# A 512-byte store ahead of the first large store on the ScalarE queue

## The chip, the core and the metric

The kernel runs on one core of one Trainium2 chip. Its time is the device time of one execution, in microseconds (us); the median of three runs is given. A profile of one execution says what each engine and each DMA queue did. The engines that matter here are ScalarE (ACT, squares and roots), VectorE (DVE, sums) and SyncE (SP, which issues most DMA transfers); the transfers themselves run on 16 DMA engines.

## The reference

The kernel is an Lp pooling with p = 2 and windows of 4: of each four neighbours along the last axis it gives the root of the mean square. The input is 32 x 256 x 4096 in float32 (134.22 MB), the output a quarter of it (33.55 MB).

```python
for i in range(out_length):
    window = np.abs(x[:, :, 4 * i:4 * i + 4]) ** p
    result[:, :, i] = np.mean(window, axis=-1) ** (1.0 / p)
```

## The kernel before

Input and output are taken as flat arrays, cut into blocks, each laid out as 128 partition rows. A load brings a tile of 128 rows by W = 13184 columns into one of three input tiles (`x_tiles`, 6592 KB a load); 20 loads cover the input, load 3 being 32 columns narrower and load 19 shorter. Six blocks of loads, `[0..3]`, `[4..7]`, `[8..11]`, `[12..15]`, `[18, 16, 17]` and `[19]`, each end in one store: store 0 holds the results of loads 0 to 3, and so on.

For each load i the work is: ScalarE squares the tile in place (`square`, L89); VectorE adds pairs (`pairs`, L95) and then pairs of these (`fours`, L99) into the output tile `ot`, or, for loads 4, 8, 12 and 16, into a PSUM tile `st`; ScalarE takes the root of a quarter of the sums (`root`, L102). The output tile has four places, one for each load of a block, and is used again by each of the first four blocks.

The order of instructions on each engine is written out by hand: there is a manual schedule, and each engine runs its own list in order. The loop at L130 gives, for each load, any roots that are due ahead of its square (`ahead`), the square, any roots due behind it (`behind`), the two sums, and then the issue of load i + 3, which goes into the input tile that has just become free. For i = 3 the roots behind the square are those of loads 0 to 2, in one instruction over 9,888 columns. For i = 4 the root of load 3 goes ahead of the square, and `roots` (L106 to L116) then calls `store(0, nc.scalar)`.

Loads are issued from SyncE's queue (L83), which the profile calls q1. Stores 0, 1 and 2 are issued from ScalarE's queue (L86), which the profile calls q10; a store stands in ScalarE's list, so squares behind it in the list are issued after it. Stores 3, 4 and 5 are issued from SyncE. Semaphores make an instruction wait for the data it needs: a load for the sums that read its tile last, a sum into `ot` for the store that reads the old results, and a DMA for an earlier DMA that writes the same bytes. DMA transfers count on eight semaphores that are handed out in turn (lanes).

Near the end some of the squares of loads 18 and 19 are done by VectorE (L155), and the last three stores follow their roots.

## Time and profile before

| what | value |
| --- | --- |
| median of 3 runs (lowest, highest) | 394.09 us (393.97, 394.21) |
| profiled execution | span 392.3 us (392.26), from first to last instruction; the page gives no other time for it |
| read from HBM, written | 134.22 MB, 33.55 MB; 428 GB/s over the span |
| ScalarE busy | 274.4 us (70%) |
| VectorE busy | 218.2 us (56%) |
| chain that ended last, shares | DMA 43%, ScalarE 30%, VectorE 23% |
| a square of a full tile, its pairs, its fours | 11.19, 7.03, 3.59 us |
| a load, one after the other (squares 1, 2 and 3 start at 34.35, 49.94 and 65.47 us) | 15.5 to 15.6 us |
| stores 0, 1, 2 from issue to landing | 36.3, 35.2 and 35.0 us, shared with loads |

The profile divides the span into 40 slices of 9.8 us; digits are tenths of busy time, and the rate row is in GB/s. In the timeline, a row gives start, length, engine, line, operation, written and read tile, and in brackets how long the engine had been idle and what ended that. In the chain of work that ended last, each row is the start and length of a piece and what it was; a piece of DMA runs from the issue of a transfer to its landing, queueing included. "issue" is time in which the engine waited for nothing that the profile shows. The letter q behind an engine's name marks its DMA queue.

### The profile page before, as it was taken

The page shows a single profiled execution, that of the slowest core. Times are in us where ns is not written, and L with a number is a line of the kernel's source. Part 1 is how long each engine was busy: PE and PEld are TensorE (multiplying, and loading weights), DVE is VectorE, ACT ScalarE, POOL GpSimd, SP SyncE. Part 2 cuts the span into 40 slices and gives each one's busy share as a digit, 9 for nine tenths or more (in the row PEclk, how much of TensorE's full clock was granted, in tenths as well). Part 3 has the DMA queues.
Part 4 walks back from the last instruction along what each step waited for, and adds up shares of the span by engine and source line. Part 5 has one row for each costly group of instructions (what it writes and reads, how often), then busy time and mean ns, then how long its engine had stood idle before and what let it go on. Part 6 is the DMA issues. An engine that isn't in the chain of part 4 may idle for free.

```text
span 392.3 us, 176 instructions
## 1 busy us (share of the span) xinstructions
DVE 218.2 (56%) x42; ACT 274.4 (70%) x37; POOL 0.2 (0%) x4
## 2 busy tenths in 40 slices
DVE  0009477580693274905942748069418485699970
ACT  1095695979950859799509597995098999969910
POOL 0000000000000000000000000000000000000000
DMA  8999999999999999999999999999999999999997
GB/s 344 430 430 430 430 440 435 452 457 366 430 430 430 430 430 430 430 441 446 452 446 441 436 430 436 430 430 430 430 430 430 430 430 430 430 453 415 430 413 342
DMA packets 3744, 167.77 MB, mean 428 GB/s; under 512 B 416, under 2 KB 416, under 8 KB 416
## 3 DMA queue, kind: packets, MB, share of 16 engines
q1 hardware_dynamic: 3312, 147.53, 87.4%
q10 hardware_dynamic: 432, 20.25, 11.9%
HBM read 134.22 MB, written 33.55 MB: 428 GB/s over the span
## 4 chain that ended last, share of the span: by engine, by line
DMA 43%; ACT 30%; DVE 23%; issue 0%; ACTq 0%; SPq 0%; DVEq 0%
DMA xt<-in_x_dram 43%; ACT xt L89 28%; DVE xt L95 14%; DVE ot L99 5%; DVE xt L99 3%; DVE xt L155 2%; ACT ot L102 2%; ACT xt L102 1%; ACTq L86 0%; SPq L83 0%; DVEq L95 0%
## 5 line engine op out<-in xcount | busy, mean ns | idle before, releaser
L89 ACT ACTIVATE xt<-xt 128x13184 f32<-128x13184 f32 (+3 forms) x20 | 216.7, 10847 | 92.3 <-DMA xt<-in_x_dram 91.0
L95 DVE TENSOR_TENSOR xt<-xt 128x6592 f32<-128x6592 f32 (+2 forms) x20 | 139.7, 6985 | 144.1 <-ACT xt L89 143.9
L99 DVE TENSOR_TENSOR ot<-xt 128x3296 f32<-128x3296 f32 (+1 forms) x13 | 46.7, 3592 | 17.9 <-DMA out_dram<-ot 17.6
L102 ACT ACTIVATE ot<-ot 128x6592 f32<-128x6592 f32 (+3 forms) x8 | 37.2, 4655 | 7.0 <-DVE ot L99 7.0
L102 ACT ACTIVATE xt<-xt 128x3296 f32<-128x3296 f32 (+1 forms) x3 | 8.5, 2836 | 8.8 <-DVE xt L99 8.8
L99 DVE TENSOR_TENSOR st<-xt 128x3296 f32<-128x3296 f32 x4 | 14.4, 3600 | 0.1
L99 DVE TENSOR_TENSOR xt<-xt 128x3296 f32<-128x3296 f32 (+1 forms) x3 | 10.4, 3461 | 0.1
L102 ACT ACTIVATE ot<-st 128x3296 f32<-128x3296 f32 x3 | 8.7, 2898 | 0.0
L155 DVE TENSOR_TENSOR xt<-xt 128x4608 f32<-128x4608 f32 (+1 forms) x2 | 7.2, 3593 | 0.0
L102 ACT ACTIVATE xt<-st 128x3296 f32<-128x3296 f32 x1 | 2.9, 2898 | 0.0
L102 ACT ACT_TABLE_LOAD x1 | 1.3, 1283 | 0.7 <-PEq L189 0.7
L102 ACT ACTIVATE first<-const-float32-1.0 128x1 f32<-128x1 f32 x1 | 0.2, 202 | 0.0
L189 POOL MEMSET const-bfloat16-1.0<- 128x1 bf16 x1 | 0.1, 101 | 0.0
L189 POOL MEMSET const-uint8-127<- 128x1 uint8 x1 | 0.1, 101 | 0.0
L189 POOL MEMSET const-float32-0.0<- 128x1 f32 x1 | 0.1, 98 | 0.2 <-issue 0.2
L189 POOL MEMSET const-float32-1.0<- 128x1 f32 x1 | 0.1, 98 | 0.0
## 6 DMA issues: line engine op xcount, KB each, us to landing
xt<-in_x_dram SPq DMA_DIRECT2D x18, 6592.0 KB, 29.8
out_dram<-ot ACTq DMA_DIRECT2D x2, 6592.0 KB, 35.1
out_dram<-ot SPq DMA_DIRECT2D x1, 6592.0 KB, 37.1
out_dram<-ot ACTq DMA_DIRECT2D x1, 6588.0 KB, 36.3
xt<-in_x_dram SPq DMA_DIRECT2D x1, 6576.0 KB, 24.7
xt<-in_x_dram SPq DMA_DIRECT2D x1, 5840.0 KB, 21.9
out_dram<-xt SPq DMA_DIRECT2D x1, 4944.0 KB, 16.1
out_dram<-xt SPq DMA_DIRECT2D x1, 1460.0 KB, 8.2
```

The costliest lines, as they stand in the source:

```text
L89: return nc.scalar.activation(out=v, in_=v, func=Act.Square)
L95: return nc.vector.tensor_tensor(out=h, in0=q[:, :, 0:2], in1=q[:, :, 2:4], op=add)
L99: return nc.vector.tensor_tensor(out=o, in0=h[:, :, 0], in1=h[:, :, 1], op=add)
L102: return nc.scalar.activation(out=o, in_=s, func=Act.Sqrt, scale=1.0 / k)
L155: nc.vector.tensor_tensor(out=v, in0=v, in1=v, op=mybir.AluOpType.mult)
L189: nc = _bacc.Bacc("TRN2", target_bir_lowering=False, num_devices=1)
```

## The change

In the turn of the loop for load 3, behind the root of loads 0 to 2 and ahead of the root of load 3, ScalarE issues one more DMA: 128 floats (512 bytes) of partition row 0 of the output tile go to the first 128 floats of the output. These are results of load 0, so the values are the right ones; store 0 writes the same bytes again with the rest of its block. ScalarE's list has one instruction more. Store 0 gets one wait more, for the small store's completion, since both write the same bytes. The lanes of all later transfers move on by one. Nothing changes in the lists of the other engines.

```diff
         for group in behind.get(i, []):
             roots(*group)
+        if i == 3:
+            nc.scalar.dma_start(out=rows(of, 0, k)[0:1, 0:128], in_=o_tile[0:1, 0:128])
         sums[i] = pairs(xs[i]), fours(summed[i], xs[i])
         if i + X_SLOTS < n:
             load(i + X_SLOTS)
```

## The prediction

> **What bounds the kernel now.** I read the page first, then the table of busy time and DMA rate by stretch, then the timeline around the edit, then the chain that ended last.

> ```profile
> span 392.3 us, 176 instructions
> ...
> DMA  8999999999999999999999999999999999999997
> GB/s 344 430 430 430 430 440 435 452 457 366 430 430 430 430 430 430 430 441 446 452 446 441 436 430 436 430 430 430 430 430 430 430 430 430 430 453 415 430 413 342
> DMA packets 3744, 167.77 MB, mean 428 GB/s; under 512 B 416, under 2 KB 416, under 8 KB 416
> ...
> q1 hardware_dynamic: 3312, 147.53, 87.4%
> q10 hardware_dynamic: 432, 20.25, 11.9%
> ```

> The DMA engines are busy in every slice while ScalarE and VectorE have gaps, so up to the last landings the transfers set the time. The packet line gives the anatomy. There are 26 transfers; 416 small packets are 16 for each, and the other 3,328 are 128 for each: one packet for each partition row, eight on each of the 16 engines, and one small completion packet an engine. q1 carries SyncE's transfers, q10 ScalarE's three stores. One figure in the rate row stands out: 366 in the tenth slice (88 to 98 us), where q10 is used for the first time.

> ```profile
> 65.47:90.30 24.83, 16.91 (x4) 22.44 (x3) 0.00 (x0) 1.00 1.01 435
> 90.30:95.30 5.00, 0.00 (x0) 4.57 (x1) 0.00 (x0) 1.00 1.02 359
> 95.30:128.86 33.56, 19.80 (x4) 17.70 (x3) 0.00 (x0) 1.00 0.99 429
> 128.86:144.41 15.55, 5.77 (x2) 11.19 (x2) 0.00 (x0) 1.00 1.00 434
> 144.41:222.22 77.81, 42.50 (x9) 55.98 (x7) 0.00 (x0) 1.00 1.00 434
> ```

> The columns are the stretch, its length, busy time of VectorE, ScalarE and GpSimd, the clock, DMA share and rate. In the 5 us behind the first store's issue the engines call themselves full yet move 359 instead of 434 GB/s. The stretch from 65.47 to 144.41 (first four rows, 78.94 us) and that from 144.41 to 222.22 (77.81 us) each hold four loads and one store. So the first use of q10 costs **1.13 us of transfer time**. The packet records agree: a row takes 1.947 us, but around 92 us each of the 16 engines has one q1 row of 2.61 to 3.11 us just ahead of its first q10 row, 0.66 to 1.16 us too much, different for each. The second and third stores show no such row.

> ```profile
> 76.54 8.43 ACT L102 ACTIVATE ot<-ot 128x9888 f32<-128x9888 f32 x1
> ...
> 83.71 3.59 DVE L99 TENSOR_TENSOR ot<-xt 128x3288 f32<-128x3288 f32 x1
> 87.33 2.94 ACT L102 ACTIVATE ot<-ot 128x3288 f32<-128x3288 f32 x1 [2.36 <-DVE ot L99]
> 90.31 0.38 ACTq L86 DMA_DIRECT2D out_dram<-ot  x1
> 90.73 22.27 ACT L89 ACTIVATE xt<-xt 128x13184 f32<-128x13184 f32 x2 [0.46 <-ACT ot L102]
> ...
> 126.71 3.59 DVE L99 TENSOR_TENSOR ot<-xt 128x3296 f32<-128x3296 f32 x1 [6.65 <-DMA out_dram<-ot]
> 128.86 11.19 ACT L89 ACTIVATE xt<-xt 128x13184 f32<-128x13184 f32 x1 [15.86 <-DMA xt<-in_x_dram]
> ```

> These are the place of the edit and what is behind it. The root of loads 0 to 2 ends at 84.97; ScalarE then idles 2.36 us until load 3's sum. Store 0 is issued at 90.31.

> ```profile
> 90.73 21.94 ACT xt L89 x2
> 112.67 31.71 DMA xt<-in_x_dram
> 144.38 0.02 issue
> ```

> The chain runs from squares 4 and 5 to load 7's issue at 112.67, but most of the 31.71 us behind it is queueing: load 7 stands behind load 6 (landed by 128.86), then takes 15.55 us of its own.

> **The change, part by part.**

> *Issue.* One more DMA instruction on ScalarE, at about 85.0. Issues there take 0.34 to 0.38 us and end inside the 2.36 us gap, so root 3 still starts at 87.33: nothing. Without the gap it would cost that 0.38 us.

> *Data.* One row of 512 bytes is, by the one-packet-a-row count, one packet on one engine, against 128 packets on 16. At a row's rate (52,736 bytes in 1.947 us) 512 bytes are 0.02 us, and a 4-byte packet takes 0.01 us. The far bound is a whole row's place, 1.95 us on that engine. I take 0.03 us, by the small packets, the nearer row.

> *The first-use stall.* No row shows a one-row store. Below, the 1.13 us vanish (-1.13); above, the small store stalls its engine and store 0 stalls all again (+1.16). I take 0. The stall sits on each engine separately and with its own length, right ahead of that engine's first q10 row, which reads as a price for each engine and queue. The small store then pays on its one engine at about 87 to 89 us, the other fifteen pay at store 0, and each pays once. An early payment is no cheaper, since the engines are full from 65.47 on, and every load needs all sixteen. Even if the other fifteen were spared, loads would wait for the one that paid. That would gain at most the spread between engines, 0.6 us at the last load, since that one may have been ahead.

> *The added wait.* Store 0 now waits for the small store's landing. The second and third stores needed 3.4 us from issue to their first row, the first 4.5. The rows of two queues alternate on an engine (3.4 plus 16 x 1.947 gives 34.6, and 35.0 to 35.2 is measured), so the completion packet comes one q1 row later. The small store lands 3.4 + 1.95 = 5.3 to 4.5 + 1.95 = 6.4 us after 85.0, at 90.3 to 91.4, and ScalarE waits 0 to 1.1 us beyond 90.31. Bounds: none at all, or 2.9 us by the shortest store on the page (1,460 KB, 8.2 us, landing at 93.2). I take 1.1. The second semaphore adds a wait instruction, 0.02 us in SyncE's rows.

> Queued behind it on ScalarE are store 0 and squares 4 and 5; behind these are the sums of loads 4 and 5, the issues of loads 7 and 8 on SyncE, and VectorE's sum at 126.71, which waits for store 0. What hides it: load 7 is issued at 112.67 and load 6 occupies q1 until 128.86; load 8 is issued at 126.71 + 3.59 = 130.30 and load 7 occupies q1 until 144.41. Take off 3.4 us of start-up, and the shorter cover is 144.41 - 130.30 - 3.4 = **10.7 us**. Store 0 starting later only lets loads 5 and 6 run faster meanwhile. So 1.1 us of wait costs nothing on the path; beyond 10.7 us every further microsecond would count. The loads' lane waits that shift by one semaphore fall on transfers that landed long before, and SyncE and GpSimd issue nothing new.

> *Sum.* 392.26 + 0.03 + 0 + 0 = 392.3 us of span. The page gives no time for the profiled execution beyond its span; the median 394.09 lies 1.8 us above it, so I forecast **394.1 us**.

> **The rivals.**

> *The stall is gone (faster).* If the first use is paid once for the whole ScalarE queue, and 512 bytes are too few to hold up the loads behind them, store 0 starts as smoothly as the second store. That gives 394.09 - 1.13 + 0.03 = 393.0 us. For it: all 16 stalls fall within 4 us, and the first store's issue is also the longest of the three (0.38 against 0.34). Against it: lengths differ by engine, and a stall of the small store on a full engine is on the path too. Chance 0.23.

> [...]

> *The stall is paid twice (slower).* [...] Chance 0.20.

> *The wait becomes the bound (slower).* If the small store took as long as store 0 did (36.3 us), it would land at 121.3, hold ScalarE 31 us, and 31 - 10.7 = 20 us would show: 414 us. Against it: those 36 us are sixteen alternating rows, and it has one. Chance 0.03.

> *It warms nothing.* All sixteen engines stall at store 0 as before: 394.1, part of the forecast.

> **How the numbers follow.** Forecast 0.54, with its own range of 393.7 to 394.5 (spread gained, or the wait's remainder). A measurement of this kernel can tell about 0.2% (0.8 us) from no change, and the forecast lies inside that; the stall gone is faster (0.23), the other two slower (0.20 + 0.03). The range takes in 393.0 and 395.0 with 0.1 to 0.2 us at each side: 392.9 to 395.2; it leaves out the long wait and the outer parts of the stall lengths.

> **What would show it.** Right: one 512-byte packet on q10 ahead of store 0; store 0 issued near 91.4; in its first 5 us still a rate near 360 GB/s; squares 7 and 11 near 144.4 and 222.2. The stall gone: about 430 GB/s there and square 7 near 143.3. [...] The wait as bound: a ScalarE wait of over 10 us at store 0. What would make it wrong: a first-use price that does not belong to each engine alone.

## The result, and the profile after

The changed kernel takes 403.88 us (402.67 to 404.28, four runs), against 394.06 us before: a ratio of 1.0245, 95% interval 1.0233 to 1.0257. The forecast was no change. The profiled execution took 404.28 us with a span of 402.5 us, 1.8 us around it as before.

The same lines of the page of the changed kernel:

```profile
span 402.5 us, 178 instructions
...
DMA  8999999999999999999999999999999999999996
...
DMA packets 3746, 167.77 MB, mean 417 GB/s; under 512 B 417, under 2 KB 418, under 8 KB 418
...
q10 hardware_dynamic: 434, 20.25, 12.4%
```

Two packets more on q10, one of data (512 bytes, 0.027 us) and one of completion (4 bytes, 0.009 us): the small store is a single row on a single engine, as forecast. The engines are still busy in every slice. They move as many bytes (167.77 MB), but at 417 instead of 428 GB/s, and the 10.2 us more of span are that.

Where the rate is lost is read from stretches between the starts of squares 3, 7, 11, 14 and 17, which wait for their loads. First the changed kernel (columns as in the prediction), then the kernel before:

```profile
65.50:150.01 84.51, 42.51 (x9) 55.90 (x6) 0.00 (x0) 1.00 1.00 406
150.01:230.65 80.64, 42.42 (x9) 55.99 (x7) 0.00 (x0) 1.00 1.00 422
230.65:294.45 63.80, 34.57 (x7) 44.80 (x6) 0.00 (x0) 1.00 1.00 423
294.45:341.19 46.74, 28.12 (x6) 44.69 (x6) 0.00 (x0) 1.00 1.00 433
```

```profile
65.47:144.41 78.94, 42.48 (x9) 55.90 (x7) 0.00 (x0) 1.00 1.00 428
144.41:222.22 77.81, 42.50 (x9) 55.98 (x7) 0.00 (x0) 1.00 1.00 434
222.22:284.49 62.27, 36.81 (x8) 44.80 (x6) 0.00 (x0) 1.00 1.00 434
284.49:331.25 46.76, 25.85 (x6) 44.70 (x7) 0.00 (x0) 1.00 1.00 433
```

The three stretches with a store on ScalarE's queue are longer by 5.57, 2.83 and 1.53 us, 9.9 of the 10.2 us; the fourth, without one, is not longer. The change touches store 0 alone, yet stores 1 and 2 are slower too. The timeline around the edit:

```profile
85.03 0.51 ACTq L144 DMA_DIRECT2D out_dram<-ot  x1
87.35 2.94 ACT L102 ACTIVATE ot<-ot 128x3288 f32<-128x3288 f32 x1 [2.36 <-DVE ot L99]
92.59 0.37 ACTq L86 DMA_DIRECT2D out_dram<-ot  x1
93.00 22.27 ACT L89 ACTIVATE xt<-xt 128x13184 f32<-128x13184 f32 x2 [2.70 <-DMA out_dram<-ot]
...
134.41 11.19 ACT L89 ACTIVATE xt<-xt 128x13184 f32<-128x13184 f32 x1 [19.14 <-DMA xt<-in_x_dram]
```

The issue at 85.03 is hidden, and root 3 starts as before. The small store lands at 92.50, so store 0 is issued at 92.59, **2.28 us** later than the 90.31 of before. Load 6 is issued by SyncE, as before, and yet lands 5.5 us later (square 6 at 134.41 instead of 128.86). The chain names the small store but not the loss:

```profile
85.03 7.48 DMA out_dram<-ot
...
93.00 21.95 ACT xt L89 x2
114.94 35.04 DMA xt<-in_x_dram
```

ScalarE's 2.3 us are passed on to load 7's issue (114.94 instead of 112.67); the rest is inside the last piece, 35.04 us instead of 31.71, although load 7 had 2.3 us less to queue.

The packet records show where the time goes. Each packet is put behind the one that ended where it starts, which gives 16 sequences, one for each engine; the records do not number the engines, and a few sequences can't be followed to their end. L is a row of a load, S of a store, c the completion packet of a load (4 bytes, 0.009 us), with start times in us and, in brackets, lengths over 2.1 us; most of the other rows take 1.947 us. Two engines before, then two after:

```
L91.9(3.1) L95.0 S96.9 c98.8 S98.9 L100.8 S102.7 L104.7 S106.6
L92.1(2.9) S95.0 L96.9 S98.9 c100.8 S100.8 L102.8 S104.7 L106.7

L91.9 L93.9(2.1) c96.0 L96.0(2.8) S98.8 L100.8 S102.7(2.1) L104.9 S106.8(2.4)
L92.2 L94.2(2.4) S96.6 c98.5 S98.5 L100.5 S102.4 L104.4 S106.3
```

Before, store 0's first row goes ahead of load 5's completion on all 16 engines. After, it still does so on one engine, and on two it comes right behind the completion; on the other 13, load 5 has ended and exactly one row of load 6 has gone ahead. Below, a store is called n rows behind on an engine when n rows of the new load stand between the old load's completion and the store's first row. The 13 engines that are one row behind are the slow ones: from the store's first row to its last, load rows between included, they take 2.2 to 2.3 us a row.

### The profile page after: what moved, and what is told of

Read it like the earlier page. It is cut to its first block, busy times and chain, and to the rows that moved or that the text cites. A ratio compares the mean times of both kernels' runs of the same rounds, so it can differ in the third digit from the quotient of the medians.

```text
span 402.5 us, 178 instructions
## 1 busy us (share of the span) xinstructions
DVE 218.2 (54%) x42; ACT 274.4 (68%) x37; POOL 0.2 (0%) x4
## 2 busy tenths in 40 slices
DMA packets 3746, 167.77 MB, mean 417 GB/s; under 512 B 417, under 2 KB 418, under 8 KB 418
## 3 DMA queue, kind: packets, MB, share of 16 engines
q1 hardware_dynamic: 3312, 147.53, 86.3%
q10 hardware_dynamic: 434, 20.25, 12.4%
## 4 chain that ended last, share of the span: by engine, by line
DMA 46%; ACT 31%; DVE 20%; issue 0%; ACTq 0%; SPq 0%; DVEq 0%
DMA xt<-in_x_dram 44%; ACT xt L89 28%; DVE xt L95 12%; DVE ot L99 4%; ACT ot L102 3%; DVE xt L99 3%; DMA out_dram<-ot 2%; DVE xt L157 2%; ACT xt L102 1%; ACTq L86 0%; SPq L83 0%; DVEq L95 0%
## 5 line engine op out<-in xcount | busy, mean ns | idle before, releaser
L89 ACT ACTIVATE xt<-xt 128x13184 f32<-128x13184 f32 (+3 forms) x20 | 216.7, 10848 | 102.4 <-DMA xt<-in_x_dram 98.9
L99 DVE TENSOR_TENSOR ot<-xt 128x3296 f32<-128x3296 f32 (+1 forms) x13 | 46.7, 3591 | 32.9 <-DMA out_dram<-ot 32.5
L102 ACT ACTIVATE ot<-ot 128x6592 f32<-128x6592 f32 (+3 forms) x8 | 37.2, 4656 | 7.0 <-DVE ot L99 7.0
L99 DVE TENSOR_TENSOR st<-xt 128x3296 f32<-128x3296 f32 x4 | 14.4, 3600 | 0.1
L102 ACT ACTIVATE xt<-xt 128x3296 f32<-128x3296 f32 (+1 forms) x3 | 8.5, 2837 | 8.6 <-DVE xt L99 8.6
L99 DVE TENSOR_TENSOR xt<-xt 128x3296 f32<-128x3296 f32 (+1 forms) x3 | 10.4, 3462 | 0.1
L102 ACT ACTIVATE ot<-st 128x3296 f32<-128x3296 f32 x3 | 8.7, 2897 | 0.0
L102 ACT ACTIVATE xt<-st 128x3296 f32<-128x3296 f32 x1 | 2.9, 2898 | 0.0
L102 ACT ACTIVATE first<-const-float32-1.0 128x1 f32<-128x1 f32 x1 | 0.2, 203 | 0.0
```

Source lines behind the costliest of these rows:

```text
L89: return nc.scalar.activation(out=v, in_=v, func=Act.Square)
L99: return nc.vector.tensor_tensor(out=o, in0=h[:, :, 0], in1=h[:, :, 1], op=add)
L102: return nc.scalar.activation(out=o, in_=s, func=Act.Sqrt, scale=1.0 / k)
```

## The experiments

They stand in the order of the questions. The kernels that only delay a store do so by short activations into unused columns of the PSUM tile, ahead of the root that the store waits for. The second diff shows the first of these kernels; the others differ in the number of activations and their columns.

**Is it the small store, or the wait for it?**

The small store goes to store 5's block, so that store 5 takes the wait over:

```diff
+        if i == 3:
+            nc.scalar.dma_start(out=rows(of, 5, k)[0:1, 0:128], in_=o_tile[0:1, 0:128])
```

> The same small store, but to the first bytes of store 5's block, so that store 5, late, has the wait and store 0 has none; everything else as in the changed kernel. Theory 'late store' (the 2.28 us by which store 0 starts later set how the 16 engines fall between load rows and store rows, and that slows all three stores): store 0 is issued near 90.3 again and the time is near before, 394 to 396 us. Rival 'one engine' (a packet on one engine puts its queue out of step with the other fifteen): 402 to 405 us, as with the change.

Measured: 394.07 us, ratio 1.0001 (0.9990 to 1.0012); store 0 was issued at 90.54. The transfer itself, 0.027 us in the changed kernel, costs nothing that shows. In the next kernel there is no small store, only the delay:

```diff
+        if i == 3:
+            for _ in range(7):
+                nc.scalar.activation(out=s_tile[:, R:R + 508], in_=o_tile[:, 0:508], func=Act.Sqrt)
```

> No small store; seven short activations ahead of the root of load 3 (into unused columns of the PSUM tile) hold ScalarE so that store 0 and square 4 come some 2.3 us later. Theory 'late store': 402 to 405 us, with rows of 2.1 us and more during all three stores on ScalarE's queue. Rival 'one engine': 394 to 395 us, since the wait has 10 us of cover.

Measured: 400.75 (profiled) and 403.82 us, ratio 1.0208 (1.0115 to 1.0300).

```profile
92.35 0.38 ACTq L86 DMA_DIRECT2D out_dram<-ot  x1
```

Store 0 is 2.0 us late, there is no small store, and most or all of the loss is there: the late store 0 is enough, and the theory of one engine falls.

**What about a late store 0 is slow?**

> As the run with 2.3 us, but store 0 only some 0.3 us later. The rows of an engine take 1.947 us, and 2.28 is one such row and 0.33 us. If the theory 'late store' goes by the place within a row, this run is slow too, 400 us or more; if it goes by the distance to the end of load 5 or by the length of the wait, 394 to 395 us. Rival 'one engine': 394 us.

Four activations of 519 columns. Measured: 394.09 us, ratio 1.0003 (0.9991 to 1.0014); store 0 at 90.48, only 0.17 us late, so this tells little.

> As the run with 2.3 us, but store 0 some 1.95 us later, one whole row. If the theory 'late store' goes by the place within a row, this run is as before, 394 us; if it goes by the end of load 5 or the length of the wait, 400 us or more. Rival 'one engine': 394 us.

Six of 574. Measured: 394.19 us in the profiled execution and 403.43 in the other, of which no trace is kept, so this decides nothing by its time. In the profile store 0 was issued at 92.17, and all 16 engines put the first store row ahead of load 5's end. At 92.35 (the kernel with seven activations) three of 16 missed it and had a row of load 6 first, and these three took 2.2 us a row, the other 13 engines 1.95. That suggested the next theory, that engines on both sides of load 5's end disturb each other.

> No small store; store 0 some 1.0 us later than before (near 91.3), between the run that was fast at 0.1 us and the ones that were slow, or now slow and now fast, at 1.7 and 2.0 us. Theory 'straddle' (slow when some engines take their first store row ahead of load 5's last completion and some behind it, fast when all sixteen are on one side): all sixteen still ahead, 394 us. Rival 'longer wait': the time grows with the lateness, so 396 to 400 us.

Five of 579. Measured: 394.21 us, ratio 1.0001 (0.9989 to 1.0014), store 0 at 91.56; all 16 ahead, as both sides of the theory "straddle" wanted.

> No small store; store 0 some 3.1 us later than before (near 93.4), later than with the change. Theory 'straddle': by now all sixteen engines finish load 5 first and begin the store behind it, so it is fast again, 394 to 395 us, though it waits longer. Rival 'longer wait': 404 us or more.

Eight of 591. Measured: 404.78 us, ratio 1.0273 (1.0243 to 1.0303), store 0 at 93.83.

```profile
95.30:125.00 29.70, 17.65 (x3) 21.22 (x2) 0.00 (x0) 1.00 1.03 391
```

The rate in this stretch is 428 GB/s in the kernel before and 383 in the changed one. Nine engines had one row of load 6 first, seven had two. "Straddle" falls: none is ahead of load 5's end, and it is slow. On the nine, a store row takes 2.28 us; on the seven, 1.95 us.

> The changed kernel, with its small store and store 0's wait for it, and besides short activations ahead of the root of load 3, so that store 0 comes some 3.1 us later than before instead of 2.3. Theory 'straddle': as the run without the small store at the same place, 394 to 395 us, 9 us faster than the changed kernel for doing more work. Rival 'longer wait': 404 us or more. If this is slow and the run without the small store fast, the small store itself has a part.

The changed kernel and seven of 623. Measured: 405.48 us in both runs, ratio 1.0291 (1.0261 to 1.0321), store 0 at 93.53. With the small store or without, about the same; here all 16 engines are one row behind load 6.

**Is it the order of load 6 and store 0?**

The changed kernel, its wait kept, with load 6 issued behind store 0:

```diff
             roots(*ahead[i])
+        if i == 4:
+            nc.scalar.activation(out=s_tile[:, R:R + 16], in_=x_tiles[0][:, 0:16], func=Act.Sqrt)
+            load(6)
...
-        if i + X_SLOTS < n:
+        if i + X_SLOTS < n and i != 3:
```

> The changed kernel with its small store and its wait, but load 6 is issued behind store 0 (a 16-column activation behind store 0's issue reads load 6's tile, and load 6 waits for it), so that store 0's first rows come ahead of load 6's though store 0 is as late as with the change. Theory 'order' (slow when load 6's rows have begun before store 0's): 394 to 396 us. Rival 'late start' (the time of the start alone, against the rest of the kernel, counts): 402 us or more.

Measured: 394.09 us in the middle of eight runs (393.80 to 394.35, and one of 399.13), ratio 1.0021 (0.9983 to 1.0058). Timeline and rate of the profiled run:

```profile
92.46 0.37 ACTq L86 DMA_DIRECT2D out_dram<-ot  x1
...
93.09 39.76 SPq L83 DMA_DIRECT2D xt<-in_x_dram  x3
```

```profile
95.30:125.00 29.70, 17.65 (x3) 19.95 (x2) 0.00 (x0) 1.00 0.98 426
```

Store 0 is as late as with the change (92.46), load 6 is issued later too, and all of the loss is gone (the execution of 399.13 us has no trace). On nine engines store 0's first row now stands ahead of load 5's completion, on seven right behind it, and its rows take 1.95 us. So it is the order of rows, not the lateness.

> No small store; store 0 some 5 us later than before, so that load 6 is two or three rows ahead of it on each engine (one or two in the slow run at 3.1 us). Theory 'order': slow, 400 to 406 us. If it is fast, it is not the order alone but how many rows load 6 is ahead.

Ten of 656, store 0 at 95.50. Measured: 394.21 us median, but from 393.76 to 403.76 over nine runs. In the profiled run (397.79 us) all 16 engines had two rows of load 6 first, and store 0's rows took 1.95 us: so "one ahead is slow" did not hold for two. Its loss came later, at store 2, which gives the clearest view of all. There one engine had one row of the new load first; on the other 15 the store began ahead of the completion. The one, and one of the 15:

```
L249.8 c251.8 L251.8 S253.9 L255.9 S257.8(2.7) L260.5 S262.4(2.7) L265.1 S267.1(2.7)
L248.1 L250.1 S252.0 c254.0 S254.0 L255.9 S257.9 L259.8 S261.8 L263.7 S265.7 L267.6
```

The one engine writes most of its rows in 2.7 us (2.54 on the mean), beside 15 that need 1.95. So the store rows go by each engine's own sequence. Where many engines are slow, though, load rows of the others grow as well: in the run with store 0 at 93.83, the seven engines that are two rows behind take 1.95 us for a store row but 2.3 us for a load row between.

> No small store; store 0 some 8 us later than before, load 6 four rows ahead of it; still inside the cover of 10.7 us. Theory 'order': slow, 400 to 406 us. The run with 128 small rows ahead of store 0 (load 6 five or six rows ahead, 394.5 us) speaks for a return to 394 to 395 us at some number of rows; this run and the one at 5 us tell where.

Fourteen of 661, store 0 at 98.55, 8.2 us late. Measured: 394.24 us, ratio 1.0010 (0.9999 to 1.0022), four rows of load 6 first on 15 engines. Waiting 8 us costs nothing; waiting 2.3 to 3.5 us costs about 10.

> The changed kernel with its small store and its wait, and activations that hold store 0 until some 8 us later than before, 6 us later than with the change. Theory 'one row behind': four rows of load 6 are ahead, so rows take 1.95 us and the time is 394 to 395 us, some 9 us faster than the changed kernel for waiting longer. Rival 'late start': 404 us or more.

The changed kernel and fourteen of 618. Measured: 394.39 us, ratio 1.0007 (0.9996 to 1.0019).

```profile
98.64 0.37 ACTq L86 DMA_DIRECT2D out_dram<-ot  x1
```

```profile
95.30:125.00 29.70, 14.26 (x3) 27.31 (x5) 0.00 (x0) 1.00 1.02 426
```

All of the change is in it, store 0 waits 6 us longer, and it is 9.5 us faster than the changed kernel; the rate of 426 GB/s is nearly the 428 of the kernel before in this stretch.

**Does it hold at another store?**

Here the activations (ten of 628, then eight of 564) stand ahead of the root of load 7, and store 0 is left alone.

> No small store, and store 0 as before; now store 1 is held some 4.8 us (near 174.1), so that on each engine its first row should come right behind exactly one row of the new load. Theory 'one row behind' (an engine is slow, rows of some 2.27 us instead of 1.947, as long as row k of a store follows row k of a load): store 0 at 1.95 us a row, store 1 slow, 398 to 403 us. Rival 'something of store 0 alone' (its place, its first-use stall, loads 5 and 6): 394 to 395 us.

Measured: 394.41 us, ratio 1.0009 (0.9998 to 1.0021). Store 1, at 174.06, came two rows behind the new load on every engine: that was one row more than intended, so it tests nothing but "two is fast".

> As the run that held store 1 by 4.8 us, which came two rows behind the new load on every engine and was fast; held by 3 us (near 172.2) it should come one row behind. Theory 'one row behind': store 0 at 1.95 us a row, store 1 at 2.2 us or more, 397 to 403 us. Rival 'something of store 0 alone': 394 to 395 us.

Measured: 404.49 us, ratio 1.0262 (1.0232 to 1.0292); somewhat more than forecast.

```profile
172.67 0.34 ACTq L86 DMA_DIRECT2D out_dram<-ot  x1
```

```profile
95.30:124.00 28.70, 17.65 (x3) 17.67 (x2) 0.00 (x0) 1.00 0.99 428
176.00:211.00 35.00, 17.65 (x3) 19.32 (x2) 0.00 (x0) 1.00 1.01 389
```

Store 0's stretch runs at 428 GB/s and store 1's at 389. Twelve engines are one row behind at store 1 and need 2.26 us for a store row. So the loss belongs to no single store, and two kernels whose store 1 is issued 1.4 us apart (172.67 and 174.06) end 10 us apart.

Over the traces of the 17 kernels that write each full store in one transfer, sequences are counted by how many rows of the new load went ahead of a store's first row on an engine. Only sequences that can be followed through the whole store count. With one, store rows take 2.24 us on the mean (some 750 rows). With none, two, three, four or five, or where the store began ahead of the load's completion, the means are 1.946 to 1.948 us (some 5,700 rows).

**Why one row?**

These four kernels have the eight activations of 591 columns of the run with store 0 at 93.83, and change store 0 besides.

> As the slow run at 3.1 us without the small store, but stores 0 and 1 write to each other's blocks of the output, both 13,176 columns wide (8 columns of a block are left out, so the output differs from the reference's). If the slowness comes from where in HBM store 0 writes relative to what loads 5 and 6 read, the time changes, most likely to 394 to 397 us; if it comes from the order alone, it stays at 402 to 406 us.

```diff
     def store(b, queue):
+        if b < 2:
+            stores[b] = queue.dma_start(out=rows(of, 1 - b, k)[:, 0:block_width[0] // k], in_=held[b][:, 0:block_width[0] // k])
+            return
```

Measured: 405.29 us, ratio 1.0285 (1.0255 to 1.0315), all 16 engines one row behind. Writing store 0 one block further on in HBM takes nothing of the loss away.

> As the slow run at 3.1 us without the small store (store 0 one row behind load 6), but store 0 goes in two transfers of 64 partitions, the upper half first. If an engine is slow because it reads from the very partition that it has just written, engine and partition no longer match and the time falls to 394 to 397 us. If the place in the sequence of rows alone counts, or the first-row position in HBM, it stays at 402 to 406 us.

```diff
+        if b == 0:
+            for a in (64, 0):
+                stores[b] = queue.dma_start(out=rows(of, b, k)[a:a + 64, :], in_=held[b][a:a + 64, :])
+            return
```

Measured: 406.67 us, ratio 1.0320 (1.0251 to 1.0390).

> As the run with the halves turned, but the lower half first. If a transfer of 64 partitions gives each engine four rows in order, engine and partition match on hardly any engine here either, and the time is again 394 to 397 us under the partition theory; if the halves stay with the engines that served them in a full transfer, this run is slow as a full store would be and only the turned one is fast, or both show eight busy engines. If the sequence alone counts: 402 to 406 us.

The same with `(0, 64)`. Measured: 406.48 us, ratio 1.0316 (1.0286 to 1.0346). Both are slow, and each half ran on all 16 engines. That speaks against the theory that an engine is slow because it reads the partition it has just written; it does not rule it out, since the records do not say which partitions an engine serves.

> As the slow run at 3.1 us without the small store, but store 0 goes in two transfers of half the columns, so its rows are half as long as load 6's. If it is the row-for-row pairing of two transfers with equal rows that is slow, the pairing is gone and it is 394 to 398 us; if any store that begins one row behind a load is slow, 402 us or more.

Two transfers of 6592 and 6584 columns. Measured: 394.71 us, ratio 1.0013 (1.0001 to 1.0024). This is inconclusive: the first half holds no result of load 3, so it did not wait for the late root and was issued at 90.01; no engine was one row behind.

**What does the first-use stall belong to?**

```diff
+        if i == 3:
+            nc.scalar.dma_start(out=rows(of, 5, k)[:, 0:128], in_=o_tile[:, 0:128])
```

> In place of the small store one of 128 rows of 512 bytes, on all 16 engines, to store 5's block, so that store 0 does not wait for it. It tells what the first-use stall of 1.13 us belongs to. If to an engine's first packet on ScalarE's queue: store 0's stretch shows none, and the long rows stand at 87 to 90 us. If to the first long store: the long rows stand at 92 to 96 us as before. The time is 393 us if it is gone, 394 us if it has only moved or stayed; over 400 us if store 0's place comes to straddle load 5's end.

Measured: 394.54 us, ratio 1.0014 (1.0003 to 1.0026). The 128 small rows passed from 90 us on without a long row beside them, and the 16 long rows of 2.5 to 3.0 us came near 104 us, just ahead of store 0's first row. The stall goes with the first long store, not with the queue's first packet.

## Why the prediction was wrong

**Right:** the small store is one packet on one engine; its issue, 0.51 us, is hidden in the 2.36 us gap; its transfer costs nothing (394.07 us in the run with the wait taken elsewhere). The bound was read rightly too: transfers set the time, since 9.9 of the 10.2 us lie in the three stretches whose squares wait for late loads.

**Right in size, not in mechanism: the first-use stall.** It is neither saved nor doubled: before, each engine has one long row, of 2.61 to 3.11 us, ahead of its first row of store 0, and after one of 2.41 to 3.24 us. So the term of 0 held. But the prediction had it paid early on the small store's engine, "at about 87 to 89 us". That engine's load rows around the small store's packet, at 90.1 us, are 1.95 us long, and its long row, 2.62 us, stands at 94.0, ahead of store 0, as on the other engines. That is "It warms nothing", which the forecast took in; the run with 128 small rows says the same of all 16 engines. Also, the long row stands just ahead of the first store row on eight engines only in the trace of before; on the other eight one ordinary load row lies between.

**The added wait, in size.** The forecast was a landing after 5.3 to 6.4 us and 1.1 us of wait; measured were 7.5 and 2.28 us, inside the bounds given (up to 8.2 and 2.9 us). The data row left at about 90.1 instead of 89.5, its completion one load row later as forecast, and store 0's wait ended some 0.4 us behind that, which the sum did not have. The size mattered only by where it put store 0: at 1.25 us (91.56) there was no loss, at 2.28 us nearly 10.

**The step that failed** is "Store 0 starting later only lets loads 5 and 6 run faster meanwhile", and with it what was concluded from the cover of 10.7 us. The sum treated the engines as conserving work: a row is 1.947 us whatever it stands between. The trace of before could not show otherwise, since in it each of the three stores begins ahead of a load's completion on every engine. With the wait, 13 engines put exactly one row of load 6 ahead of store 0 and need 2.2 to 2.3 us a row. From the store's first row to its last there are 15 rows, eight of the store and seven of the load; at 0.35 us more on the slowest engines they are 5.3 us, against 5.57 measured in the first stretch. A load lands with its slowest engine: load 6's completions run from 129.48 to 134.08 us, where before they ran from 127.83 to 128.48, and square 6 starts at 134.41. After that the engines no longer end their loads together (load 7's completions lie 4.61 us apart, against 0.65 before), and at stores 1 and 2 five engines each time are one row behind. That goes with the other 2.83 and 1.53 us, but no sum was made for them. The cover was real, as the runs with 8 us of lateness show (394.24 and 394.39 us); it covers waiting, not a change in the order of rows.

**The rivals.** "The wait becomes the bound" had the right part of the change and the wrong mechanism: its point was 10.7 us and its price a microsecond for each beyond. The real loss starts near 2 us of lateness (400.75 us with store 0 at 92.35) and is gone at 8 us (394.24 us). "The stall is paid twice" fell, since the rows around the small store's packet are of ordinary length (1.95 us), and "The stall is gone" fell, since each engine has its long row still. No run shows the second stall that 395.0 us in the range stands for; the runs showed one long row on each engine in its place.

**Left open:** why an engine whose store is one row behind a load is slower by 0.3 us a row (2.24 against 1.947), and why load rows of other engines grow beside many such engines (2.3 us with nine of them). It is shown that the store rows go engine by engine (2.54 us beside 1.95 at store 2, with store 0 at 95.50), that this holds at all three stores, and that it stays with another place in HBM (405.29 us). Halves of partitions in either order did not change it (406.67 and 406.48 us). Whether rows of equal length are needed was not settled.

## What to carry to other kernels

A wait that has plenty of cover can still cost, if a transfer behind it changes its place among the rows of another queue: here 2.28 us of wait with 10.7 us of cover cost 9.8 us. When two queues share engines that are always full, look at which row stands ahead of which, not only at the slack. Where such an order decides, holding the other transfer as well can help where the wait can't be shortened: here load 6 behind store 0 took back all of the 10 us, with the wait kept (394.09 us). The "harmless" transfer to bytes that a later store rewrites was not harmless here, because the later store waited for its landing, 7.5 us for 512 bytes.
